# Norm statistics' matmuls between the first pairs' products, operand sums ahead of plain pairs, pools in another order of addresses

## Chip, cores and metric

The kernel runs on one core of one Trainium2 chip. The metric is the device time in microseconds (us); lower is better. TensorE is called PE, VectorE DVE, ScalarE ACT, GpSimd POOL and SyncE SP.

## What is computed

One layer of a decoder trunk over 512 tokens and a width of 1024, in float32: half a SwiGLU feed-forward block (FFN1), token mixing by a convolution branch and a spatial-gating branch, cross-attention over 256 memory tokens, half a second feed-forward block (FFN2), and a final norm.

```python
def rms_norm(x, g):
    xf = x.astype(jnp.float32)
    y = xf * lax.rsqrt(jnp.mean(xf * xf, axis=-1, keepdims=True) + EPS_RMS)
    return (y * g.astype(jnp.float32)).astype(x.dtype)

def swiglu(x, w_gu, w_down):
    gu = x @ w_gu
    g, u = jnp.split(gu, 2, axis=-1)
    return (jax.nn.silu(g) * u) @ w_down
...
  h = x + 1/2 * SwiGLU_1(RMSNorm(x))
  n = RMSNorm(h);  P = n @ W_in + b_in
  A: GLU -> causal depthwise conv (width 31) -> LayerNorm(channels) -> swish -> proj to D
  B: GELU -> split u,v -> LayerNorm(v) -> chunked (128) causal spatial gating u * (W_s v + b), 4 head groups -> proj to D
  merge: sigmoid(gate_A) * y_A + sigmoid(gate_B) * y_B  -> W_out
  h = h + merged
  h = h + CrossAttn(RMSNorm(h), RMSNorm_mem(mem))
  h = h + 1/2 * SwiGLU_2(RMSNorm(h))
  y = RMSNorm_final(h)
```

## The kernel before

**Number format.** The hidden state `h` lies in SBUF, channels on partitions: 8 tiles of 128 channels x 512 tokens. A float32 operand is split into a high part and a low remainder in a shorter format: the high part is a cast on ACT, the low part a subtraction on DVE (`split`, `split_scaled`, lines 190 to 196, and line 110 for weights). One product of the mathematics is then three matmuls (`mm3`, lines 116 to 119: high x high, high x low, low x high), so "a product" below means one of these 128x512 matmuls. Names that end in h and l are the two parts.

**The norms.** `rstat` (lines 211 to 231) makes a norm's factor. ACT squares each tile of `h` and DVE adds it into `acc` (`add_square`, line 204). On PE, n?c (line 218) sums `acc` over channels, as tokens on partitions; DVE adds epsilon (n?m, line 220); POOL takes the power -1/2 (n?r, line 208); DVE scales an identity by it (n?d, line 224); on PE, n?b (line 226) spreads the factors over all partitions; ACT copies them to SBUF (n?rb, line 230). The question mark is 1 in FFN1, 2 ahead of the mixing stage, 3 ahead of the attention, 4 in FFN2. Each n? therefore makes PE wait for DVE, POOL and DVE between its two matmuls, unless other products stand there.

**An FFN.** The width of 2816 is worked in 22 blocks: 6 plain ones (`plain_up`, line 290, `pl` the gate and up sums, `pw0` to `pw5` the weights) and 16 by a Strassen-like scheme of fewer products (`double_f`), whose operands (`operands`) are sums of quarters of the normed x. The first two plain blocks (in FFN1 called `f`, with weights `fw`) are multiplied on x before its norm, and rb is applied to their sums afterwards (`plain_f`, with rb, lines 302 to 309); the others take the normed x (`normed`, line 329: `xf`, `xg`, `lb`, then their split into `xh` and `xl`). In FFN1 the squares are summed after the first blocks' products were issued; in FFN2 `rstat` for n4 is called once after the attention and again inside `ffn`.

**The middle.** Memory keys (`pk`, `kt`), the n2 norm, the conv branch's projections (`av`, `ag`) and its convolution in steps on DVE (line 606), the gating branch, values (`pv`), the branch outputs (`ya`, from `aa`, and `yb`), `w_out` (sums `o`, line 805 adds them to `h`), n3, then queries (`pq`), scores, weighted values and `w_o` (`wo`, line 888). Linear layers fetch weights through a ring (`wpool`) and split them.

**What sets the order.** A scheduler at build time orders the instructions of each engine by its own model of their times, under the data's dependences, the tile pools (a tile of a ring waits for the readers of the one it replaces) and the stages: `stage` opens a list of pools, one behind the other in address, and a tile of a new pool waits only for the old tiles that lay at its addresses. The order of the list therefore decides what a stage's first loads and casts wait for. The middle has one pool `big` of 50 tiles of 128x512 for everything. PSUM has 6 banks for products and 2 for the small ones (n?c, n?b). Each engine's instructions, and SP's DMA issues, run in the order given.

Of the kernel before, what the change touches and what calls it, by code (L numbers as in the profile page):

```python
# [54 lines left out]
def conformer_layer(ctx: ExitStack, tc: tile.TileContext, xT, memT, vecs, rows, w_gp1, w_gs1, w_dn1, w_in_f, w_in_t,  # L55
# [22 lines left out]
    per.tile([P, 24], F32, name="fill")  # L78
# [156 lines left out]
    def slot(name, dt=F32):  # L235
        return pool["big"].tile([P, T], dt, tag="s", name=name, bufs=50)

    def pair(name):
        return slot(name + "h", F32R), slot(name + "l", F32R)
# [6 lines left out]
    FFN_POOLS = ("xops", "wp", "wt", "wr", "wtt", "fp", "tmp")  # L246
# [232 lines left out]
    def ffn(firsts, g, acc, nm, w_gp, w_gs, w_dn, done, last=None):  # L479

        tf, pf = t8("xf"), pt6("xg", F32)
        _, rb = rstat([acc], T, EPS_RMS, nm)
# [12 lines left out]
        if NPL // 2 - 1 in after:  # L495
            down(w_dn, after[NPL // 2 - 1], fs, lambda m: None)
        for d in range(NPL // 2, FT // 2):
            fs[d] = new_f(d)
# [277 lines left out]
    for i in range(DT):  # L776
# [81 lines left out]
    def transposed(pr):  # L858
        out = []
        for j in range(MT):  # L860
# [8 lines left out]
    def weighted(hd, p):  # L869
        for i in range(HT):  # L870
# [170 lines left out]
```

## Time and profile before

| quantity | value |
|---|---|
| median of 3 runs | 1358.31 us (1355.76 to 1358.43) |
| the profiled execution's own time | 1357.26 us |
| its span | 1355.5 us |
| PE busy in the span | 1298.0 us, 96% |
| DVE busy | 903.0 us, 67% |
| ACT busy | 610.9 us, 45% |
| POOL busy | 63.3 us, 5% |
| mean granted clock of PE | 0.975 |

The span is cut from the profiled execution; 1.8 us of its time lie around it. Busy times are sums over instructions. The granted clock is 1 at PE's full speed. A row of a timeline gives the start, the duration, the engine and line, what was written from what, and in brackets how long the engine had been idle and what released it. A matmul's listed duration overlaps with the next one's, so the pace is read from one start to the next.

### The profile page before, as it was taken

To read this page: it belongs to the slowest core of one execution; us is meant where nothing else is said; L and a number is where in the kernel's file an instruction comes from. 1 tells how busy PE (TensorE), PEld (TensorE's weight loads), DVE (VectorE), ACT (ScalarE), POOL (GpSimd) and SP (SyncE) were. 2 spreads that over 40 slices of the span, in tenths; PEclk is the share of its full clock that TensorE was granted. 3 is DMA by queue.
4 is the path that set the end of the run, shared out by engine and by line. 5 is a ranking of instruction groups with operands and counts; after the bars stand their busy time and mean duration, and the time that the engine had idled before them with its cause. 6 is when DMAs were issued, how large, how long until landed. Compare 5 with 4: busy or idle time off the path is not lost.

```text
span 1355.5 us, 17560 instructions
## 1 busy us (share of the span) xinstructions
PE 1298.0 (96%) x7082; PEld 1124.8 (83%) x7082; DVE 903.0 (67%) x1285; ACT 610.9 (45%) x837; POOL 63.3 (5%) x80
## 2 busy tenths in 40 slices
PE   7799999999989999999999999999879999999996
PEld 5589898989878888888888788887658899999995
DVE  4656575665577999999986785555444647575645
ACT  6454554545443223243225643334345455455533
POOL 1000000000020000100000000000111000000000
PEclk9799999999999999999999999999879999999998
DMA  8465565565443222332333333202355546574631
GB/s 250 103 166 131 145 160 163 133 172 129 150 149 116 94 94 95 101 108 80 94 106 113 94 120 96 64 24 67 124 125 125 171 110 172 128 182 130 165 93 62
DMA packets 39809, 166.19 MB, mean 123 GB/s; under 512 B 4337, under 2 KB 7153, under 8 KB 34353
## 3 DMA queue, kind: packets, MB, share of 16 engines
q1 hardware_dynamic: 32096, 129.17, 30.1%
q0 software_dynamic: 7632, 35.92, 13.9%
q8 instruction: 55, 0.90, 0.3%
q14 instruction: 26, 0.20, 0.0%
HBM read 162.97 MB, written 2.10 MB: 122 GB/s over the span
## 4 chain that ended last, share of the span: by engine, by line
PE 74%; issue 14%; DMA 6%; DVE 3%; ACT 2%; POOL 0%; SPq 0%; POOLq 0%; DVEq 0%; ACTq 0%
PE d L117 3%; PE d L118 3%; PE d L119 3%; PE r L186 2%; PE r L187 2%; PE r L185 2%; PE pl L118 2%; PE pl L119 2%; PE pl L117 2%; PE av L118 1%; PE ya L118 1%; PE ya L117 1%; PE av L119 1%; PE ya L119 1%; PE yb L117 1%
## 5 line engine op out<-in xcount | busy, mean ns | idle before, releaser
L606 DVE SCALAR_TENSOR_TENSOR cv<-ap,vec,cv 128x497 f32<-128x497 f32 (+27 forms) x240 | 163.9, 730 | 1.3 <-ACT cv L604 0.9
L242 DVE SCALAR_TENSOR_TENSOR h<-d,h 128x512 f32<-128x512 f32 x79 | 53.8, 687 | 22.8 <-PE d L119 22.2
L203 ACT ACTIVATE sq<-h 128x512 f32<-128x512 f32 x34 | 21.0, 623 | 25.7 <-DVE h L242 16.4
L312 DVE TENSOR_TENSOR u<-pl,g 128x512 f32<-128x512 f32 x8 | 5.5, 690 | 31.8 <-PE pl L119 31.8
L204 DVE TENSOR_TENSOR acc<-acc,sq 128x512 f32<-128x512 f32 x34 | 23.3, 686 | 4.1 <-ACT sq L203 3.7
L196 DVE SCALAR_TENSOR_TENSOR xl<-h,vec,xh 128x512 fp32r<-128x512 f32 x16 | 11.4, 744 | 5.4 <-ACT xh L195 5.4
L117 PE MATMUL pl<-xh,pw20h 128*128 128x512 f32 x16 | 8.6, 563 | 6.4 <-ACT xh L191 6.4
L220 DVE TENSOR_SCALAR n4m<-n4c 128x4 f32<-128x4 f32 x2 | 0.3, 157 | 21.4 <-PE n4c L218 21.4
L805 DVE TENSOR_TENSOR h<-o,h 128x512 f32<-128x512 f32 x8 | 5.5, 692 | 12.5 <-PE o L119 12.5
L794 DVE TENSOR_TENSOR ga<-ya,sga 128x512 f32<-128x512 f32 x8 | 5.5, 690 | 11.9 <-PE ya L119 11.9
L192 DVE TENSOR_TENSOR s40tl<-s40t,s40th 128x1024 fp32r<-128x1024 f32 x4 | 4.9, 1226 | 12.6 <-ACT s40th L191 12.6
L192 DVE TENSOR_TENSOR s60tl<-s60t,s60th 128x1024 fp32r<-128x1024 f32 x4 | 4.9, 1225 | 12.5 <-ACT s60th L191 12.5
L888 DVE TENSOR_TENSOR h<-wo,h 128x512 f32<-128x512 f32 x8 | 5.4, 688 | 11.6 <-PE wo L119 11.6
L192 DVE TENSOR_TENSOR dn40l<-dn,dn40h 128x768 fp32r<-128x768 f32 x4 | 3.8, 959 | 13.2 <-ACT dn40h L191 13.2
L192 DVE TENSOR_TENSOR s80tl<-s80t,s80th 128x1024 fp32r<-128x1024 f32 x4 | 4.9, 1226 | 11.6 <-ACT s80th L191 11.6
L192 DVE TENSOR_TENSOR s100tl<-s100t,s100th 128x1024 fp32r<-128x1024 f32 x4 | 4.9, 1225 | 11.4 <-ACT s100th L191 11.4
L117 PEld LDWEIGHTS pl<-xh,pw20h 128*128 128x128 f32 x16 | 4.3, 281 | 9.8 <-ACT xh L191 8.9
L191 ACT CAST s31th<-s31t 128x1024 fp32r<-128x1024 f32 x4 | 4.2, 1052 | 17.5 <-PE d L118 17.5
L117 PE MATMUL pl<-xh,pw30h 128*128 128x512 f32 x16 | 7.4, 490 | 4.6 <-DVE g L306 4.6
L195 ACT ACTIVATE xh<-h,vec 128x512 fp32r<-128x512 f32 x16 | 10.9, 713 | 1.4 <-PE wo L119 0.9
L191 ACT CAST fh<-u 128x512 fp32r<-128x512 f32 x12 | 7.4, 618 | 8.8 <-DVE u L309 8.8
L118 PE MATMUL pl<-xl,pw20h 128*128 128x512 f32 x16 | 8.2, 515 | 3.1 <-DVE xl L192 3.1
(3770 smaller groups left out, 5072.3 us busy)
## 6 DMA issues: line engine op xcount, KB each, us to landing
s<-w_gs SPq DMA_DIRECT2D x32, 1024.0 KB, 5.6
dn<-w_dn SPq DMA_DIRECT2D x32, 512.0 KB, 3.9
pw<-w_gp SPq DMA_DIRECT2D x10, 1024.0 KB, 5.1
dn<-w_dn SPq DMA_DIRECT2D x8, 768.0 KB, 5.0
h<-xT SPq DMA_DIRECT2D x8, 256.0 KB, 7.4
first<-w_gp SPq DMA_DIRECT2D x4, 512.0 KB, 7.6
r10w<-w_in_t SPq DMA_DIRECT2D x4, 512.0 KB, 3.7
r11w<-w_in_t SPq DMA_DIRECT2D x4, 512.0 KB, 3.8
```

Of the source, the lines that this page charges most:

```text
L117: PE.matmul(out, whi, ahi, start=start, stop=False)
L118: PE.matmul(out, whi, alo, start=False, stop=False)
L119: PE.matmul(out, wlo, ahi, start=False, stop=stop)
L185: PE.matmul(accs[t], a_h, whi[:, k - k0, :], start=k == 0, stop=False)
L186: PE.matmul(accs[t], a_h, wlo[:, k - k0, :], start=False, stop=False)
L187: PE.matmul(accs[t], a_l, whi[:, k - k0, :], start=False, stop=k == nk - 1)
L191: S.copy(out=hi, in_=src)
L192: V.tensor_tensor(out=lo, in0=src, in1=hi.bitcast(F32), op=ALU.subtract)
L203: S.activation(sq, src, AF.Square)
L204: V.tensor_tensor(out=acc, in0=acc, in1=sq, op=ALU.add)
L242: V.scalar_tensor_tensor(out=h[:, m, ts], in0=pd, scalar=0.5, in1=h[:, m, ts], op0=ALU.mult, op1=ALU.add)
L606: V.scalar_tensor_tensor(out=o, in0=aps[i][:, :T - back], scalar=w, in1=o, op0=ALU.mult, op1=ALU.add)
```

## The change

It splits `rstat` in two, `rstat_cols` (n?c to n?d) and `rstat_rows` (n?b and its copy), so that products can stand between them. In FFN1 the squares are added inside the loop over channels, n1c comes ahead of the last channel tile's products, n1b between the two blocks of the last tile, and a third plain block (`pw2`) is multiplied on the x before its norm. In FFN2, n4c goes between the two halves of the first plain block and n4b between those of the second, and the other call for n4 is dropped. The operands' sums are made ahead of the first plain block that takes the normed x, no longer behind it. The middle's pools are regrouped: `xp`, `kv` (8 tiles for keys, values, csum and later the probabilities) and `tmp` live through the whole middle; `mixing` (`big` with 34 tiles, `mp` with 8, `wpool`) is closed after n3 and `attention` (`big` with 26, `late` with 16, `wpool`) opened in its place. The FFN's pools get an order each.

```diff
-    def rstat(accs, n, eps, name, copy=True):
+    def rstat_cols(accs, n, eps, name):
...
+        return rc, dg
+
+    def rstat_rows(dg, n, name, copy=True):
+
         pb = ps2.tile([P, T], F32, tag="st", name=name + "b")[:, :n]
         PE.matmul(pb, ones, dg, start=True, stop=True)
...
-    FFN_POOLS = ("xops", "wp", "wt", "wr", "wtt", "fp", "tmp")
+
+    FFN1_POOLS = ("wr", "fp", "wtt", "tmp", "xops", "wp", "wt")
+    FFN2_POOLS = ("wp", "fp", "tmp", "wr", "wtt", "xops", "wt")
...
-    def plain_up(w_gp, j, xh, xl, by_dma):
+    def plain_up(w_gp, j, xh, xl, by_dma, between=None):
...
             plain_mm(accs, w, xh, xl, kh, range(4))
+            if kh == 0 and between is not None:
+                between()
         return accs
...
-        fs = {0: new_f(0)}
-        for j in range(2):
-            plain_f(firsts[j], rb, fs[0], j)
-        for j in range(2, NPL):
+        fs = {}
+        ops = None
+        for j in range(NPL):
             if j % 2 == 0:
                 fs[j // 2] = new_f(j // 2)
+            if j < len(firsts):
+                plain_f(firsts[j], rb, fs[j // 2], j % 2)
+                continue
+            if ops is None:
+                ops = operands(x, src)
             plain_f(plain_up(w_gp, j, xh, xl, True), None, fs[j // 2], j % 2)
-            if j == 2:
-                ops = operands(x, src)
...
+            if k == DT - 2:
+                add_square(acc, h[:, k + 1, :], False)
+                dg = rstat_cols([acc], T, EPS_RMS, "n1")[1]
             for j in range(2):
                 plain_mm(firsts[j], ws[j], xh, xl, kh, (0, 1) if kk == 1 else (kk,))
-        acc = new_acc("acc0")
-        for k in range(DT):
-            add_square(acc, h[:, k, :], k == 0)
+                if k == DT - 1 and j == 0:
+                    rb = rstat_rows(dg, T, "n1")
+        firsts.append(plain_up(w_gp1, 2, xh, xl, True))
...
-    stage(middle, ("wpool", "xp", "big", "tmp"), 5)
+    stage(middle, ("xp", "kv", "tmp"), 5)
+    mixing = ExitStack()
+    stage(mixing, ("big", "mp", "wpool"), 5)
+    SLOTS.update(big=34, mp=8, kv=8)
...
     rc, rb = rstat([acc], T, EPS_RMS, "n3")
     acc = new_acc("acc3")
 
+    mixing.close()
+    attention = ExitStack()
+    stage(attention, ("big", "late", "wpool"), 5)
+    SLOTS.update(big=26, late=16)
...
-    _, rb = rstat([acc], T, EPS_RMS, "n4")
+    attention.close()
     middle.close()
...
-        firsts = [plain_up(w_gp2, j, xh, xl, False) for j in range(2)]
+        stat = []
+        firsts = [plain_up(w_gp2, 0, xh, xl, False, lambda: stat.append(rstat_cols([acc], T, EPS_RMS, "n4")[1]))]
+        firsts.append(plain_up(w_gp2, 1, xh, xl, False, lambda: stat.append(rstat_rows(stat[0], T, "n4"))))
+        rb = stat[1]
```

What the scheduler makes of it is shown at three places. In the rows x4 is a count, and what stands in front of MATMUL is the line.

**PE in FFN1, at n1.** Before, n1c and n1b stand side by side behind the last `f`:

```order
L118 MATMUL f_126<-xl_107,fw11h 128x512
L119 MATMUL f_126<-xh_104,fw11l 128x512
L218 MATMUL n1c<-avg,acc_255 128x1 x4
L226 MATMUL n1b<-n1d,ones 128x512
L117 MATMUL pl_347<-xh_300,pw20h 128x512
L117 MATMUL pl_348<-xh_300,pw20h 128x512
L117 MATMUL pl_455<-xh_300,pw30h 128x512
L117 MATMUL pl_456<-xh_300,pw30h 128x512
L118 MATMUL pl_347<-xl_301,pw20h 128x512
```

With the change, n1c stands 24 products ahead of the last `f`:

```order
L118 MATMUL f_126<-xl_106,fw11h 128x512
L119 MATMUL f_126<-xh_103,fw11l 128x512
L218 MATMUL n1c<-avg,acc_127 128x1 x4
L117 MATMUL f_123<-xh_104,fw01h 128x512
L118 MATMUL f_123<-xl_107,fw01h 128x512
```

and n1b stands behind the fifth product of the third block:

```order
L119 MATMUL f_126<-xh_104,fw11l 128x512
L117 MATMUL pl_298<-xh_101,pw20h 128x512
L118 MATMUL pl_298<-xl_105,pw20h 128x512
L119 MATMUL pl_298<-xh_101,pw20l 128x512
L117 MATMUL pl_298<-xh_101,pw20h 128x512
L118 MATMUL pl_298<-xl_105,pw20h 128x512
L230 MATMUL n1b<-n1d,ones 128x512
L119 MATMUL pl_298<-xh_101,pw20l 128x512
```

n1c and n1b now have 24 and 5 products between them; before they had none, and 43 products of the third block follow n1b before the first normed xh.

**PE and DVE where the attention begins.** Before, PE goes from the last `o` to `pq`; n3c stands further on, among the products of `pq0` and `pq1`. DVE makes the low parts of `pq2` and `pq3` there:

```order
L118 MATMUL o_6926<-mg7l,o7w0h 128x512
L119 MATMUL o_6926<-mg7h,o7w0l 128x512
L117 MATMUL pq_7014<-xhi,pq0w0h 128x512
L118 MATMUL pq_7014<-xlo,pq0w0h 128x512
L119 MATMUL pq_7014<-xhi,pq0w0l 128x512
```

```order
L805 TENSOR_TENSOR h<-o_6926,h 128x512
L110 TENSOR_TENSOR pq2w0l<-pq2w_7089,pq2w0h 128x1024
L196 SCALAR_TENSOR_TENSOR xlo<-h,vec,xhi 128x512
L204 TENSOR_TENSOR acc_6699<-acc_6699,sq 128x512
L110 TENSOR_TENSOR pq3w0l<-pq3w_7170,pq3w0h 128x1024
L220 TENSOR_SCALAR n3m<-n3c 128x4
```

With the change, n3c stands ahead of `pq`, and on DVE the low parts of the keys (`k0l`, `k1l`) ahead of the last `xlo` and `acc`:

```order
L118 MATMUL o_6934<-mg7l,o7w0h 128x512
L119 MATMUL o_6934<-mg7h,o7w0l 128x512
L218 MATMUL n3c<-avg,acc_6707 128x1 x4
L117 MATMUL pq_7034<-xhi,pq0w0h 128x512
L118 MATMUL pq_7034<-xlo,pq0w0h 128x512
L119 MATMUL pq_7034<-xhi,pq0w0l 128x512
```

```order
L830 TENSOR_TENSOR h<-o_6934,h 128x512
L192 TENSOR_TENSOR k0l<-kt_3400,k0h 128x512
L192 TENSOR_TENSOR k1l<-kt_3515,k1h 128x512
L196 SCALAR_TENSOR_TENSOR xlo<-h,vec,xhi 128x512
L204 TENSOR_TENSOR acc_6707<-acc_6707,sq 128x512
L192 TENSOR_TENSOR k2l<-kt_3580,k2h 128x512
L110 TENSOR_TENSOR pq0w0l<-pq0w_7035,pq0w0h 128x1024
L220 TENSOR_SCALAR n3m<-n3c 128x4
```

n3c moved ahead of the 35 products of `pq` that stood in front of it; the keys' and the values' splits, which on DVE followed the last `mg` early in `w_out`'s products, came behind the last `h`, and so did `pq0`'s.

**PE from `w_o` into FFN2.** Before, the first n4c stands between the last `wo` and the first `pl`:

```order
L118 MATMUL wo_7919<-oo7l,wo7w0h 128x512
L119 MATMUL wo_7919<-oo7h,wo7w0l 128x512
L218 MATMUL n4c<-avg,acc_6981 128x1 x4
L117 MATMUL pl_8022<-xh_7997,pw00h 128x512
L118 MATMUL pl_8022<-xl_8001,pw00h 128x512
L117 MATMUL pl_8023<-xh_7997,pw00h 128x512
```

With the change it stands behind 29 products of `pw0`, and n4b behind 43 more:

```order
L118 MATMUL pl_8026<-xl_8006,pw01h 128x512
L119 MATMUL pl_8026<-xh_8003,pw01l 128x512
L117 MATMUL pl_8026<-xh_8003,pw01h 128x512
L118 MATMUL pl_8026<-xl_8006,pw01h 128x512
L218 MATMUL n4c<-avg,acc_6989 128x1 x4
L119 MATMUL pl_8026<-xh_8003,pw01l 128x512
```

```order
L118 MATMUL pl_8101<-xl_8006,pw10h 128x512
L119 MATMUL pl_8101<-xh_8002,pw10l 128x512
L230 MATMUL n4b<-n4d,ones 128x512
L117 MATMUL pl_8100<-xh_8003,pw11h 128x512
L118 MATMUL pl_8100<-xl_8006,pw11h 128x512
```

The second pair of n4c and n4b, which stood behind all 96 products, is gone; 24 products follow n4b before the first normed xh.

## Rows read from the trace of the kernel before

**Rows 1.** Page, sections 1 and 6: PE's busy time; the pw loads.

```profile
PE 1298.0 (96%) x7082; PEld 1124.8 (83%) x7082; DVE 903.0 (67%) x1285; ACT 610.9 (45%) x837; POOL 63.3 (5%) x80
...
pw<-w_gp SPq DMA_DIRECT2D x10, 1024.0 KB, 5.1
```

**Rows 2.** Waits of PE: engine line <- releaser: us in total, times, longest.

```profile
PE pl L117 <- ACT xh L191: 6.4, 2, 3.2
PE n4c L218 <- DVE acc L204: 6.1, 1, 6.1
PE pl L117 <- DVE g L306: 4.6, 2, 2.3
...
PE n1b L226 <- DVE n1d L224: 2.9, 1, 2.9
...
PE n4b L226 <- DVE n4d L224: 2.4, 1, 2.4
...
PE pk L117 <- ACT m0h L195: 1.9, 1, 1.9
PE ya L117 <- ACT aa0h L191: 1.9, 1, 1.9
```

**Rows 3.** Stretches: us; busy us (xcount) of PE, PEld, DVE, ACT, POOL; PEclk, DMA share, GB/s.

```profile
30.90:51.90 21.00, 11.09 (x28) 6.73 (x27) 15.51 (x26) 10.90 (x14) 2.83 (x3) 0.59 0.57 142
...
376.20:412.00 35.80, 30.04 (x184) 26.83 (x184) 28.63 (x54) 17.99 (x33) 7.57 (x11) 0.86 0.55 176
...
440.00:714.50 274.50, 274.41 (x1269) 228.50 (x1268) 260.01 (x378) 87.76 (x110) 4.29 (x5) 1.00 0.31 95
...
752.20:760.00 7.80, 5.92 (x18) 4.15 (x17) 6.56 (x10) 7.80 (x14) 0.00 (x0) 0.78 0.73 217
...
962.80:1015.00 52.20, 36.63 (x133) 27.84 (x132) 26.38 (x43) 22.65 (x28) 7.61 (x6) 0.77 0.56 155
```

**Rows 4.** Timeline of PE, FFN1's norm: start us, us, engine line op [idle before <-releaser].

```profile
30.65 0.39 PE L119 MATMUL f<-xh,fw11l 128*128 128x512 f32 x1
30.88 0.95 PE L218 MATMUL n1c<-avg,acc 128*128 128x1 f32 x8
34.73 2.00 PE L226 MATMUL n1b<-n1d,ones 128*128 128x512 f32 x2 [2.90 <-DVE n1d L224]
...
46.35 0.80 PE L118 MATMUL pl<-xl,pw20h 128*128 128x512 f32 x1 [1.53 <-DVE xl L192]
46.95 0.63 PE L119 MATMUL pl<-xh,pw20l 128*128 128x512 f32 x1
47.37 0.63 PE L117 MATMUL pl<-xh,pw20h 128*128 128x512 f32 x1
```

**Rows 5.** Timeline of DVE, same stretch.

```profile
20.61 0.68 DVE L204 TENSOR_TENSOR acc<-acc,sq 128x512 f32<-128x512 f32 x1
...
37.38 2.74 DVE L329 SCALAR_TENSOR_TENSOR xf<-h,vec,n1rb 128x512 f32<-128x512 f32 x4 [2.71 <-ACT n1rb L230]
...
45.08 2.35 DVE L192 TENSOR_TENSOR xl<-xf,xh 128x1024 fp32r<-128x1024 f32 x2
```

**Rows 6.** Timeline of PE, from the attention's last product into FFN2.

```profile
962.78 0.39 PE L119 MATMUL wo<-oo7h,wo7w0l 128*128 128x512 f32 x1
...
1010.77 0.79 PE L118 MATMUL pl<-xl,pw20h 128*128 128x512 f32 x1 [1.53 <-DVE xl L192]
```

**Rows 7.** Line 208 (POOL): duration ns min/median/max, first and last start.

```profile
L208 POOL TENSOR_TENSOR n4r<-n4m,vec x2: 1030/2010/2990, 972.3 to 997.8; 128x4 f32<-128x4 f32 x2
...
L208 POOL TENSOR_TENSOR n2r<-n2m,vec x1: 1009/1009/1009, 393.3 to 393.3; 128x4 f32<-128x4 f32 x1
```

**Rows 8.** Timeline of PE where pq begins.

```profile
843.42 0.39 PE L117 MATMUL pq<-xhi,pq0w0h 128*128 128x512 f32 x1
```

**Rows 9.** Timeline of DVE at the last h of the mixing stage.

```profile
843.62 0.69 DVE L805 TENSOR_TENSOR h<-o,h 128x512 f32<-128x512 f32 x1 [2.05 <-PE o L119]
...
846.33 0.68 DVE L204 TENSOR_TENSOR acc<-acc,sq 128x512 f32<-128x512 f32 x1
```

More of the change, by code (lines that the diff above doesn't have):

```diff
@@ L76, in conformer_layer @@
     G.memset(mhalf, -0.5)
-    per.tile([P, 24], F32, name="fill")
+    per.tile([P, 8], F32, name="fill")
     pool = {}
@@ L227, in rstat, with slot, pair @@
         if not copy:
-            return rc, pb
+            return pb
         rb = per.tile([P, n], F32, tag=f"rb{n}", name=name + "rb", bufs=1)
         S.copy(out=rb, in_=pb)
-        return rc, rb
+        return rb
+    def rstat(accs, n, eps, name, copy=True):
+        rc, dg = rstat_cols(accs, n, eps, name)
+        return rc, rstat_rows(dg, n, name, copy)
     def new_acc(name):
         return per.tile([P, T], F32, tag="acc", name=name, bufs=1)
[L235 to L239, printed above, removed]
+    SLOTS = {}
+    def slot(name, dt=F32, of="big"):
+        return pool[of].tile([P, T], dt, tag="s", name=name, bufs=SLOTS[of])
+    def pair(name, of="big"):
+        return slot(name + "h", F32R, of), slot(name + "l", F32R, of)
     def add_half(m, pd, ts=slice(0, T)):
         V.scalar_tensor_tensor(out=h[:, m, ts], in0=pd, scalar=0.5, in1=h[:, m, ts], op0=ALU.mult, op1=ALU.add)
-    FFN_POOLS = ("xops", "wp", "wt", "wr", "wtt", "fp", "tmp")
+    FFN1_POOLS = ("wr", "fp", "wtt", "tmp", "xops", "wp", "wt")
+    FFN2_POOLS = ("wp", "fp", "tmp", "wr", "wtt", "xops", "wt")
     def raw2(name):
@@ L505, in conformer_layer @@
     with ExitStack() as stack:
-        stage(stack, FFN_POOLS, 7)
+        stage(stack, FFN1_POOLS, 7)
         HF = DT // 2
@@ L520, in conformer_layer @@
         ws = {}
+        acc = new_acc("acc0")
         for k in range(DT):
             split_scaled(xh[k], xl[k], h[:, k, :], col("ffn1_norm", k))
+            if k < DT - 1:
+                add_square(acc, h[:, k, :], k == 0)
             kh, kk = k // HF, k % HF
@@ L564, in mem_operands @@
             if k % 2 == 0:
-                hi, lo = pair(f"m{k0 + k}")
+                hi, lo = pair(f"m{k0 + k}", "mp")
             c = slice(k % 2 * NM, (k % 2 + 1) * NM)
@@ L632, in conformer_layer @@
                     channel_multiplier=-1)
-    wsh, wsl = pair("ws")
+    wsh, wsl = pair("ws", "kv")
     split(wsh, wsl, wsr)
@@ L660, in norm_v @@
         for t in range(TT):
-            st = pool["tmp"].tile([P, 2, 6], F32, tag="st6", name="st", bufs=2)
+            st = pool["tmp"].tile([P, 2, 6], F32, tag="st6", name="st", bufs=1)
             for half in range(2):
@@ L664, in norm_v @@
                 yield OP_US
-            mv = pool["tmp"].tile([P, 2], F32, tag="mv", name="mv", bufs=2)
+            mv = per.tile([P, 2], F32, tag="mv", name="mv", bufs=2)
             V.bn_aggr(out=mv, in_=st)
@@ L718, in value @@
         for t in range(MT):
-            vts[t][half] = slot(f"vt{half}{t}")
+            vts[t][half] = slot(f"vt{half}{t}", of="kv")
             S.activation(vts[t][half], accs[t], AF.Copy, scale=mrc[:, t:t + 1])
@@ L782, in conformer_layer @@
         V.tensor_tensor(out=y, in0=y, in1=sg, op=ALU.mult)
-        hi, lo = pair(f"aa{i}")
+        hi, lo = pair(f"aa{i}", "mp" if i < 4 else "big")
         split(hi, lo, y)
@@ L863, in transposed @@
                 PE.transpose(pt[:, t * P:(t + 1) * P], pr[t][:, j * P:(j + 1) * P], ident)
-            hi, lo = pair("p")
+            hi, lo = pair("p", "kv")
             split(hi, lo, pt)
@@ L875, in weighted @@
                 mm3(po, vh[j][k // 4][:, kc], vl[j][k // 4][:, kc], p[j][0], p[j][1], j == 0, j == MT - 1)
-            hi, lo = pair(f"oo{k}")
+            hi, lo = pair(f"oo{k}", "late")
             split(hi, lo, po)
@@ L916, in conformer_layer @@
         attn_out(m, 0, 8)
-    _, rb = rstat([acc], T, EPS_RMS, "n4")
+    attention.close()
     middle.close()
     with ExitStack() as stack:
-        stage(stack, FFN_POOLS, 7)
+        stage(stack, FFN2_POOLS, 7)
         xh, xl = plain_x()
```

15 lines of the change are left out of this document (7 added, 8 removed).

## The prediction

> **What bounds the kernel now.** I read the page first: TensorE (PE) is busy for 1298.0 of 1355.5 us [rows 1], so what can be won is what PE still waits, and what it does at half clock. Next the waits of PE [rows 2]: the reader is to see that the long ones sit in few places. The two FFNs' norms have xh (6.4 us, two waits), g (4.6, two), n4c (6.1), n1b (2.9) and n4b (2.4); besides, pk waits 1.9 for m0h and ya 1.9 for aa0h. Third, the stretches [rows 3]. Where PE waited, its clock fell from 1.00 to a mean of 0.59 (30.9 to 51.9 us) or 0.77 (962.8 to 1015): PE ran there partly at 1.2 instead of 2.4 GHz. Between 440 and 714.5 us it lacks nothing. Last the timelines: a product of 128x512 follows the one before after 0.23 us at full clock and after 0.42 us at half [rows 4].
>
> **FFN1's norm (n1).** Now PE stands from n1c at 30.88 to the first xl product at 46.35 with little to do [rows 4]: 15.5 us, in which its own work is n1c 0.95, n1b about 1.0 (it took 2.00 at half clock) and four products by 0.23, so 2.9. In the change n1c stands 24 products earlier, at 30.88 - 24 x 0.23 = 25.4. Its sum is ready at 20.61 + 0.68 = 21.3 [rows 5], so it does not wait. From n1c's end to n1b was 2.9 us [rows 4]; n1b now has 29 products in front of it (6.7 us), so it doesn't wait either and starts at 25.4 + 0.95 + 6.7 = 33.0. From n1b's start to the first xl took 11.6 us, 10.6 without the 1.0 that n1b ran long. That makes 43.6. PE meanwhile has n1b, 43 products of the third pair (9.9) and the four xh products: 44.8. So xl is there first, by 1.2 us; the chain xf to xl on VectorE (DVE), 37.38 to 45.08 [rows 5], lies beside the third pair. Wait gained: 15.5 - 2.9 = **12.6**. The half clock goes with it: 46.35 to 51.9 ran at half, 5.5 us, half of which is **2.8**. The third pair's two more multiplications by rb are DVE work in a stretch where DVE has 5.5 us idle [rows 3], and cost nothing; without that cover they cost two instructions like acc's, 1.4. Together **-15.4**.
>
> **FFN2's norm (n4).** From the last product of w_o, 962.78 + 0.23 = 963.0, to the first xl product at 1010.77 [rows 6] are 47.8 us. In the change PE goes straight from w_o into pw0, n4c stands behind 29 products, at 963.0 + 6.7 = 969.7. The last sum into acc, which came 6.1 us late [rows 2] behind a run of xl on DVE, stands in the new order right behind the last h, xl and squares being spread over w_o's last products. n4c takes 0.95, 43 products 9.9, so n4b starts at 980.5; the chain's 2.9 is covered. The second n4c and n4b, and their waits, are gone. After n4b PE has 1.0 + 24 x 0.23 + 4 x 0.23 and is through at 987.9. The normed xl comes 10.6 after n4b's start, and n4rb stands behind the casts of pw3 on ScalarE (ACT), about 0.7 more (an estimate from half of the queue that the order shows): 991.8. So there remains a wait of some 3.9, most of it the four products' on xh, g and xl, and a stretch at half clock behind it as now. 991.8 against 1010.77 is **-19.0**; with no wait at all it would be -22.9, with the queue's whole two casts in the way -17.5.
>
> **Where the attention begins.** Here the change adds a wait. pq starts now at 843.42 without one [rows 8]. In the new order n3c stands ahead of the first pq, and the sum that it needs is behind more work: DVE has k0l, k1l (their tiles lie in the pool opened only here), then xlo, then acc. The last h is added at 843.62 and takes 0.69 [rows 9]; four instructions of about 0.6 behind it end at 846.7. PE idles from 843.4 to 846.7, 3.3 us. pq0w0h is cast behind the last xhi, square and k2h, and its low half behind that, so the third product waits another 0.5 or so. What is behind n3c in PE's queue is all of pq. n3c itself only moves. After such waits half clock follows: in 752.2 to 760, behind a wait of 1.9, the mean is 0.78, so (1 - 0.78) / 0.5 x 7.8 = 3.4 us at half, 1.7 lost [rows 3]; I take 1.9 here. Sum **+5.7**; the ends are 3.3 (no fall of the clock) and 9 (a clock loss as long as that of 376.2 to 412, below).
>
> **Into the middle, and pv to ya.** From 376.2 to 412 PE lacks 35.8 - 30.0 = 5.8 us, and at mean clock 0.86 it loses 5.0 more [rows 3]. mem's casts and squares now stand ahead of the last down casts, so pk's 1.9 goes [rows 2] with some 1.7 of clock; in return d waits for its own casts about 1.5, and n2c, now directly behind nmb, leaves n2b little cover of its 2.9 us chain, 1.1 more. **-1.0**, between -5 (most of the 10.8 gone) and +3 (every wait comes back longer). At ya, aa0h moves up on ACT: 0.5 of its 1.9 goes, and the clock's 1.7: **-2.2**, between 0 and -3.6.
>
> Weighed at n2b: POOL's power (line 208) took 1.03 us for one n4r and 2.99 for the other, and 1.01 for n2r [rows 7]. Between n2's mean and its diagonal the new order has only the kt products on DVE, which read PSUM; I take 1.0, and the other end adds 2.0. The Trainium skill (SBUF — State Buffer, § Who interferes with whom) says that a DVE instruction with two SBUF inputs and a GpSimd one that reads SBUF shut each other out; kt has one such input, so by it, too, n2r stays short, and the sum would be as here; by the 2.99 of the trace it would be 2.0 higher.
>
> **The rest.** The products' number is the same but for the duplicate statistics. Sizes and order of pools leave FFN bodies and tail as they are; the operands' sums ahead of pw3 are DVE work with the plain pairs over it. 0.
>
> **Sum:** -15.4 - 19.0 + 5.7 - 1.0 - 2.2 = **-31.9**. The profiled execution took 1357.26 (span 1355.5 and 1.8 around it); that makes 1325.4. The median shown is 1.05 above that execution, so **1326**.
>
> **Rivals.**
> 1. *Loads come late.* The pools opened for the attention and FFN2 lie over tiles in use until just before. pw0's load is now queued on SP ahead of w_o's last, and its cast ahead of two w_o casts on ACT; if its tile comes free late, all three wait. Price: a load, 5.1 [rows 1], and clock of 1.9, in one place: 1333; in both 1340. For it: the load waits for PE. Against it: w_o's last four products, 4 x 24 x 0.23 = 22 us, run meanwhile. Chance 0.15.
> 2. *The new waits are cheaper.* No clock loss at pq (-1.9) and the middle's better end (-4): 1320. Chance 0.15.
> 3. *Slower: the mixing stage starves.* It keeps 34 shared tiles and 8 for mem and aa where 50 were. If a tile that a gate or a projection needs comes free only when the conv is through, DVE stands and the sums behind it come late. DVE is busy 260.0 of 274.5 us there [rows 3], and PE is at its limit, so the first few us are hidden. To end slower by 0.2% DVE would have to idle 35 us more than now, a busy share under 0.84 instead of 0.95 in that stretch: 1361. Against it: the same instructions stand there, and conv steps come earlier than now against v's norm. Chance 0.03.
> 4. *The norm's gain is given back* by one miss in both FFNs, for instance PSUM banks freed late by g and u: 30 us back, no change, 1357. Chance 0.02.
>
> **How the numbers follow.** 0.65 for the forecast, with bounds of its own terms of 1320 to 1332. 1316 to 1340 takes in both nearer rivals and the terms' ends. About 0.2% (2.7 us) is what a measurement of this kernel can tell from no change: faster 0.95, same 0.02, slower 0.03.
>
> **What would show it.** Right: n1c and n1b wait for nothing, clock 1.00 from 31 to 52 us; one n4c and one n4b, without waits; one new wait of PE, n3c on acc, near 3.3 us; about 4 us left in FFN2's xh, g, xl. Wrong: a wait of wo or pq on a weight cast; DVE below 0.84 in the conv; pl of FFN1 waiting for xl.

## The result and the profile after

The change takes 1321.34 us, median of 4 runs (1318.53 to 1323.13), against 1358.37 for the kernel before (4 runs, 1355.76 to 1359.5): the ratio is 0.973, 95% interval 0.971 to 0.975, so 37.0 us less. The forecast was 1326: 31.9 less than the profiled execution of before, and 1.05 added because the median of before lay above that execution. The profiled execution of the change took 1321.24, with a span of 1319.1.

The page's line of the engines, after (against [rows 1]: PE has 14 us less busy time for all but ten of the same matmuls; some 2 us of that are the ten, the second n4c and n4b, and the rest goes with the mean granted clock, which rose from 0.975 to 0.988):

```profile
PE 1284.0 (97%) x7072; PEld 1117.5 (85%) x7072; DVE 903.5 (68%) x1282; ACT 610.5 (46%) x836; POOL 59.8 (5%) x79
```

First, where the gain arises. These are rows of PE's timeline before: the last product of FFN1's plain blocks (`pl`, called FFN1's last up product below), the first `av`, the first `ya`, the last `o`, the last `pl` of FFN2 (FFN2's last up product) and the last 512-column product of its down sums `d`. The last `wo` stands in [rows 6]:

```profile
91.47 0.39 PE L119 MATMUL pl<-xh,pw51l 128*128 128x512 f32 x1
...
402.26 0.50 PE L117 MATMUL av<-xhi,av0w0h 128*128 128x512 f32 x1 [1.54 <-ACT xhi L191]
...
754.46 0.50 PE L117 MATMUL ya<-aa0h,yaw0h 128*128 128x512 f32 x1 [1.88 <-ACT aa0h L191]
...
843.19 0.39 PE L119 MATMUL o<-mg7h,o7w0l 128*128 128x512 f32 x1
...
1055.02 0.39 PE L119 MATMUL pl<-xh,pw51l 128*128 128x512 f32 x1
...
1335.52 0.39 PE L119 MATMUL d<-fh,dn43l 128*128 128x512 f32 x1
```

and the same after, with the last `wo`:

```profile
76.12 0.39 PE L119 MATMUL pl<-xh,pw51l 128*128 128x512 f32 x1
...
384.55 0.50 PE L117 MATMUL av<-xhi,av0w0h 128*128 128x512 f32 x1 [2.11 <-ACT xhi L191]
...
734.03 0.39 PE L117 MATMUL ya<-aa0h,yaw0h 128*128 128x512 f32 x1
...
822.20 0.39 PE L119 MATMUL o<-mg7h,o7w0l 128*128 128x512 f32 x1
...
946.63 0.39 PE L119 MATMUL wo<-oo7h,wo7w0l 128*128 128x512 f32 x1
...
1019.97 0.39 PE L119 MATMUL pl<-xh,pw51l 128*128 128x512 f32 x1
...
1299.93 0.39 PE L119 MATMUL d<-fh,dn43l 128*128 128x512 f32 x1
```

The differences, from place to place, against the terms of the prediction (negative: earlier with the change, time won):

| up to | after - before, us | of it in this piece | term |
|---|---|---|---|
| FFN1's last up product | -15.35 | -15.35 | -15.4 |
| first `av` | -17.71 | -2.36 | -1.0 |
| first `ya` | -20.43 | -2.72 | -2.2 |
| last `o` | -20.99 | -0.56 | 0 |
| last `wo` | -16.15 | +4.84 | +5.7 |
| FFN2's last up product | -35.05 | -18.90 | -19.0 |
| FFN2's last down product | -35.59 | -0.54 | 0 |
| end of the span (1355.5, 1319.1) | -36.4 | -0.8 | 0 |

The longest waits of PE that are left (engine line <- releaser: us in total, times, longest) follow. Left out are those that the kernel before has too at the start and in the final norm, FFN2's two, whose rows stand further down, and those under 1.4. Against [rows 2], the waits of n4c, n1b and n4b, both on xh, pk's and ya's 1.9 are gone, and one is new, n3c's:

```profile
PE n3c L218 <- DVE acc L204: 3.3, 1, 3.3
...
PE av L117 <- ACT xhi L191: 2.1, 1, 2.1
PE av L118 <- DVE xlo L192: 2.0, 1, 2.0
...
PE n2b L230 <- DVE n2d L224: 1.4, 1, 1.4
```

The stretches after (columns as in [rows 3]; the first is FFN1's norm, the second the way into the middle, the third the conv, the fourth pv to ya, the fifth the start of pq, the sixth FFN2's norm):

```profile
30.90:51.90 21.00, 21.00 (x92) 16.85 (x91) 17.04 (x26) 15.91 (x20) 3.52 (x4) 1.00 0.95 219
362.00:398.00 36.00, 30.48 (x189) 26.87 (x189) 25.16 (x46) 14.12 (x22) 6.81 (x11) 0.91 0.58 176
427.00:702.00 275.00, 275.00 (x1273) 229.24 (x1272) 259.21 (x379) 90.11 (x114) 4.28 (x5) 1.00 0.31 97
732.00:748.00 16.00, 15.23 (x66) 12.04 (x65) 13.63 (x19) 14.80 (x24) 0.00 (x0) 1.00 0.49 138
...
822.40:841.90 19.50, 16.16 (x59) 12.84 (x59) 13.67 (x22) 9.45 (x14) 1.33 (x1) 0.82 0.36 109
...
946.60:980.00 33.40, 30.57 (x123) 23.91 (x122) 16.19 (x28) 16.77 (x20) 4.64 (x5) 0.90 0.57 125
```

FFN1's norm lacks nothing any more: PE is busy for all of 30.9 to 51.9, at clock 1.00 where it was 0.59. The conv's DVE share is 259.2 of 275, 0.94 against 0.95: rival 3 didn't come.

PE at FFN1's norm: n1c, n1b and the first product on the normed x.

```profile
25.48 0.95 PE L218 MATMUL n1c<-avg,acc 128*128 128x1 f32 x8
...
32.97 1.02 PE L230 MATMUL n1b<-n1d,ones 128*128 128x512 f32 x2
...
43.62 0.61 PE L117 MATMUL pl<-xh,pw30h 128*128 128x512 f32 x2
```

The prediction had 25.4 and 33.0 for the first two, and the normed xl ready (43.6) before the third block ends (44.8). No row has an idle time in brackets.

PE from `w_o` into FFN2:

```profile
953.43 0.95 PE L218 MATMUL n4c<-avg,acc 128*128 128x1 f32 x8
...
964.10 1.02 PE L230 MATMUL n4b<-n4d,ones 128*128 128x512 f32 x2
...
972.95 1.39 PE L117 MATMUL pl<-xh,pw30h 128*128 128x512 f32 x2 [1.89 <-DVE g L321]
975.27 0.80 PE L118 MATMUL pl<-xl,pw20h 128*128 128x512 f32 x1 [0.94 <-DVE xl L192]
```

Counted from the end of the last `wo` (946.63 + 0.23 = 946.86): n4c at 6.6 (predicted 6.7), n4b at 17.2 (17.5), the first xl product at 28.4 (28.8).

Where pq begins, on PE, behind the last `o` of 822.20:

```profile
825.92 1.50 PE L218 MATMUL n3c<-avg,acc 128*128 128x1 f32 x8 [3.34 <-DVE acc L204]
827.28 0.77 PE L117 MATMUL pq<-xhi,pq0w0h 128*128 128x512 f32 x1
```

and on DVE, whose `acc` n3c waits for:

```profile
822.62 0.69 DVE L830 TENSOR_TENSOR h<-o,h 128x512 f32<-128x512 f32 x1 [2.61 <-PE o L119]
823.23 0.68 DVE L192 TENSOR_TENSOR k0l<-kt,k0h 128x512 fp32r<-128x512 f32 x1
823.83 0.69 DVE L192 TENSOR_TENSOR k1l<-kt,k1h 128x512 fp32r<-128x512 f32 x1
824.43 0.75 DVE L196 SCALAR_TENSOR_TENSOR xlo<-h,vec,xhi 128x512 fp32r<-128x512 f32 x1
825.09 0.68 DVE L204 TENSOR_TENSOR acc<-acc,sq 128x512 f32<-128x512 f32 x1
```

The wait is 3.34 (predicted 3.3), and the chain is the predicted one.

### The profile page after: what moved, and what is told of

The parts are those of the page before. It is cut to its first block, busy times and chain, and to the rows that moved or that the text cites. A ratio compares the mean times of both kernels' runs of the same rounds, so it can differ in the third digit from the quotient of the medians.

```text
span 1319.1 us, 17537 instructions
## 1 busy us (share of the span) xinstructions
PE 1284.0 (97%) x7072; PEld 1117.5 (85%) x7072; DVE 903.5 (68%) x1282; ACT 610.5 (46%) x836; POOL 59.8 (5%) x79
## 4 chain that ended last, share of the span: by engine, by line
PE 76%; issue 14%; DMA 6%; DVE 3%; ACT 1%; POOL 0%; DVEq 0%; POOLq 0%; SPq 0%
PE d L117 4%; PE d L119 4%; PE d L118 4%; PE r L186 2%; PE r L187 2%; PE r L185 2%; PE pl L118 2%; PE pl L119 2%; PE pl L117 2%; DMA s60pl<-w_gs 1%; PE pq L117 1%; PE av L118 1%; PE pq L118 1%; PE pq L119 1%; PE av L119 1%
## 5 line engine op out<-in xcount | busy, mean ns | idle before, releaser
L631 DVE SCALAR_TENSOR_TENSOR cv<-ap,vec,cv 128x497 f32<-128x497 f32 (+29 forms) x240 | 163.3, 727 | 1.5 <-ACT cv L629 0.9
L191 ACT CAST s31th<-s31t 128x1024 fp32r<-128x1024 f32 x4 | 4.2, 1052 | 17.5 <-PE d L118 17.5
L208 POOL TENSOR_TENSOR rs<-va,vec 128x1 f32<-128x1 f32 x4 | 3.7, 933 | 168.9 <-DVE va L693 168.9
L858 DVE TENSOR_TENSOR qt<-pq,n3rb 128x512 f32<-128x512 f32 x8 | 5.5, 691 | 8.2 <-PE pq L119 8.1
L117 PE MATMUL f<-xh,fw00h 128*128 128x512 f32 x8 | 3.7, 501 | 7.7 <-ACT fw00h L191 7.7
L195 ACT ACTIVATE xhi<-h,vec 128x512 fp32r<-128x512 f32 x8 | 5.8, 720 | 11.5 <-DVE h L830 11.5
L192 DVE TENSOR_TENSOR fl<-u,fh 128x512 fp32r<-128x512 f32 x12 | 8.2, 685 | 3.8 <-ACT fh L191 3.8
L192 DVE TENSOR_TENSOR dn41l<-dn,dn41h 128x768 fp32r<-128x768 f32 x4 | 3.8, 953 | 10.2 <-ACT dn41h L191 10.2
L878 ACT ACTIVATE pr<-sc,mx 128x256 f32<-128x256 f32 x16 | 7.4, 471 | 6.8 <-DVE mx L875 6.8
```

The source lines that it names most:

```text
L117: PE.matmul(out, whi, ahi, start=start, stop=False)
L192: V.tensor_tensor(out=lo, in0=src, in1=hi.bitcast(F32), op=ALU.subtract)
L195: S.activation(hi, src, AF.Copy, scale=g)
L631: V.scalar_tensor_tensor(out=o, in0=aps[i][:, :T - back], scalar=w, in1=o, op0=ALU.mult, op1=ALU.add)
```

## The experiments

Where a run is said to be ahead or late "at the last `o`" or another product, the starts of that product in the profiled executions are compared, as in the table above. PE's first wait, for fw00h, was 6.9 to 8.5 us in these executions, so a difference under 1.5 us at one place says little.

### The three parts alone: e1, e2, e3

e1: FFN1's code alone. The pools, the operands' sums and FFN2 stay as before.

```diff
         for k in range(DT):
...
+            if k < DT - 1:
+                add_square(acc, h[:, k, :], k == 0)
...
+                dg = rstat_cols([acc], T, EPS_RMS, "n1")[1]
...
+                if k == DT - 1 and j == 0:
+                    rb = rstat_rows(dg, T, "n1")
+        firsts.append(plain_up(w_gp1, 2, xh, xl, True))
```

> FFN1's part of the change alone (squares inside the loop, n1c and n1b between products, a third plain pair ahead of the norm), with the pools, the middle and FFN2 as before. Theory (the wait is gone because 29 products stand between n1c and n1b and 43 behind n1b; addresses have no part in it): PE clock 1.00 from 31 to 52 us, FFN1 15.4 us shorter, the rest as before: -15.4 us against before, ratio 0.9887. Rival (the new addresses are needed, since pw2's load or its tiles come free too late in the old order): a wait of PE on pw20h or pw30h in FFN1, less than 10 us won.

Measured: 1336.45 against 1355.83, ratio 0.987 (0.985 to 0.988). At FFN1's last up product it is 15.4 ahead of before, as the change is. n4c's wait of 6.1 stays. Ahead of the first `ya` it gains 6.3 more, though pk's wait is still there; that piece is looked at in the last section.

e2: FFN2's code alone, with the old pools.

```diff
-    _, rb = rstat([acc], T, EPS_RMS, "n4")
...
+        firsts = [plain_up(w_gp2, 0, xh, xl, False, lambda: stat.append(rstat_cols([acc], T, EPS_RMS, "n4")[1]))]
+        firsts.append(plain_up(w_gp2, 1, xh, xl, False, lambda: stat.append(rstat_rows(stat[0], T, "n4"))))
```

> FFN2's code alone (n4 once, n4c and n4b inside the first two pairs), with the pools and FFN1 as before. Theory (what starts the pairs early is the order of addresses, not the code): n4c still stands right behind the last wo and still waits 6 us on acc, with half clock behind it; the second n4c and n4b and their 2.4 us go, and the chain behind n4b is partly covered: -8.5 us, ratio 0.9937. Rival (the code alone moves the statistics): the whole -19.

e3: the pools alone, with the old code of both norms.

```diff
+    FFN1_POOLS = ("wr", "fp", "wtt", "tmp", "xops", "wp", "wt")
+    FFN2_POOLS = ("wp", "fp", "tmp", "wr", "wtt", "xops", "wt")
...
+    stage(middle, ("xp", "kv", "tmp"), 5)
+    stage(mixing, ("big", "mp", "wpool"), 5)
...
+    stage(attention, ("big", "late", "wpool"), 5)
```

> The pools alone (the three stages' order of addresses, the middle regrouped), with n1, n4 (twice) and the operands' sums as before. Theory: at FFN2 the wait of 6.1 on acc and its half clock go (about -10), where the attention begins n3c waits 3.3 with half clock behind (+5), ahead of the projections and at ya some 5 are won: -10, ratio 0.993. Rival (addresses hardly matter, the code of the norms does it all): within 3 us of before.

Measured: e2 1343.88, ratio 0.991 (0.989 to 0.993); e3 1345.36, ratio 0.993 (0.991 to 0.994). e2's profiled execution took 1347.31, 3.4 more than its median. Between the last `wo` and FFN2's last up product e2 gains 10.3 and e3 8.9; the change gains 18.9. So that term has two halves of nearly equal size. What each half is, the rows show. In e2, which has FFN2's new code, n4c still stands right behind the last `wo`, on PE:

```profile
962.87 0.39 PE L119 MATMUL wo<-oo7h,wo7w0l 128*128 128x512 f32 x1
969.36 1.84 PE L218 MATMUL n4c<-avg,acc 128*128 128x1 f32 x8 [6.11 <-DVE acc L204]
```

It waits as in the kernel before, because `acc` stands behind seven xl on DVE:

```profile
963.90 4.71 DVE L196 SCALAR_TENSOR_TENSOR xl<-h,vec,xh 128x512 fp32r<-128x512 f32 x7
```

In e3, which has the old code, n4c stands behind 29 products of `pw0`, as in the change, and waits for nothing:

```profile
960.25 0.39 PE L119 MATMUL wo<-oo7h,wo7w0l 128*128 128x512 f32 x1
...
967.06 0.95 PE L218 MATMUL n4c<-avg,acc 128*128 128x1 f32 x8
```

and the last `acc` on DVE ends 2.3 behind the last `wo`, where it ends 6.1 behind it in e2:

```profile
962.13 0.69 DVE L204 TENSOR_TENSOR acc<-acc,sq 128x512 f32<-128x512 f32 x1 [0.76 <-ACT sq L203]
```

So it is the pools, and not the new code, that put products ahead of n4c and `acc` early. With the new addresses pw0's first cast starts at 938.2 in e3, 22 us ahead of the last `wo`'s end; with the old ones it starts at 965.6 in e2, 2.5 behind it, so that no product on it could follow the last `wo` directly. FFN2's code gives the other half: the second n4c and n4b are gone, and n4b stands behind 72 products instead of 28, so that it and FFN2's xh are waited for no longer. e3 also has the new n3c wait of 3.3, and loses 4.7 between the last `o` and the last `wo` as the change does (4.8): that loss belongs to the pools.

The three spans are 20.5, 9.9 and 11.6 shorter than before, 42.0 together against the change's 36.4. The difference lies in the middle: up to the last `o` e1 gains 6.2 beyond FFN1, e3 7.1, and the change 5.6. e1's edit touches nothing there, and its gain is in large part clock (last section); that the change could not win this on top of e3's is argued, not shown.

### Two un-normed blocks in FFN1: e4

```diff
-        firsts.append(plain_up(w_gp1, 2, xh, xl, True))
```

> The change without the third plain pair ahead of n1. Theory (that pair is the cover of the chain from n1b to the normed xl, 10.6 us): PE waits about 9 us on xh, g and xl in FFN1 again, half clock behind it costs some 3 more: 1332 us, 11 us above the change. Rival (n1c's early place won the time, the pair only moved work): within 3 us of the change.

Measured: 1333.47, ratio 0.984 (0.983 to 0.985). FFN1's last up product is only 1.4 ahead of before; 13.9 of the 15.4 are gone, or 13.1 of 15.8 if one counts from PE's first product, which came 0.8 later in e4 than in the change. PE in FFN1, where the third block's products were:

```profile
38.56 1.22 PE L117 MATMUL pl<-xh,pw20h 128*128 128x512 f32 x2 [4.54 <-ACT xh L191]
...
42.06 1.40 PE L117 MATMUL pl<-xh,pw30h 128*128 128x512 f32 x2 [2.28 <-DVE g L321]
...
45.65 0.79 PE L118 MATMUL pl<-xl,pw20h 128*128 128x512 f32 x1 [2.20 <-DVE xl L192]
```

Moving n1c and n1b takes away their own 2.9, but the chain behind n1b (rb, xf, xh, xl) is as long as ever, and PE waits for it at the next place. The cover of 48 more products (the third block) is what wins the time.

### The wait ahead of pq: e5, e6

e5: one weight ring for the whole middle, opened ahead of the mixing stage, so that pq0's load and casts need not wait for a pool opened only there. To make room, the orders of the FFNs' pools change too.

```diff
-    FFN1_POOLS = ("wr", "fp", "wtt", "tmp", "xops", "wp", "wt")
+    FFN1_POOLS = ("wr", "fp", "tmp", "xops", "wtt", "wp", "wt")
...
-    stage(middle, ("xp", "kv", "tmp"), 5)
+    stage(middle, ("xp", "kv", "tmp", "wpool"), 5)
...
-    stage(mixing, ("big", "mp", "wpool"), 5)
+    stage(mixing, ("big", "mp"), 5)
...
-    stage(attention, ("big", "late", "wpool"), 5)
+    stage(attention, ("late", "big"), 5)
```

> The change with the weight ring (wpool) opened once for the whole middle instead of anew for the attention, and the FFN's pools put in an order that fits. Theory (the wait of n3c comes from the ring that was opened anew: pq's first casts must wait until w_out is through, so pq can't go ahead of n3c): PE goes from the last o straight into pq, n3c stands among pq's products and waits for nothing, no half clock there: 4.9 us below the change, 1316.5, ratio 0.969. Rival (the keys' splits ahead of xlo and acc on DVE make the wait): the 3.3 us stay, 1321.

Measured: 1321.15, ratio 0.974 (0.972 to 0.976): no different from the change, a miss for the 1316.5 of theory, and yet the wait is gone. PE goes from the last `o` into pq:

```profile
826.39 0.39 PE L119 MATMUL o<-mg7h,o7w0l 128*128 128x512 f32 x1
826.62 0.39 PE L117 MATMUL pq<-xhi,pq0w0h 128*128 128x512 f32 x1
```

From the last `o` to the end of pq0 it wins 4.8 on the change, what theory gave. But it came to `o` 4.2 late: n2b now waits 4.0, where the change has 1.4. In this layout the squares of the memory are summed later on DVE (nmc at 376.6 instead of 370.2), and all of kt's six multiplications, 2.07 us, then stand between n2's mean and its diagonal. The loss is not in the place that the edit was for, but in another whose tiles share the same addresses; whether FFN1's order or the ring's place puts the squares later was not separated.

e6: the keys' and values' splits written behind the first query, to see whether k0l and k1l make the wait.

```diff
+    fill(0)
     kh, kl = [], []
...
-    for i in range(3):
+    for i in range(1, 3):
```

> The change with the keys' and values' splits written behind the first query. Theory (the ring makes the wait, two splits of 0.6 only lengthen it): n3c waits about 2.1 instead of 3.3, half clock behind it stays: 1 to 1.5 us below the change, ratio about 0.972. Rival (the splits are the cause): the whole 4.9 go, ratio 0.969.

Measured: 1322.26, ratio 0.975 (0.973 to 0.976); n3c waits 3.0 instead of 3.3. Neither theory's 2.1 and its gain of 1 to 1.5 came, nor the rival's 4.9: without the keys ahead of it, `acc` is hardly earlier. In the change's trace ACT makes the square that `acc` adds from 823.98 to 824.59, behind xhi (823.35) and the last `h`; so `acc` can't start before 824.6, against 825.09, and only 0.5 of the 3.3 is the keys'. Nor would n3c further back have won the rest: ACT casts pq0w0h from 825.00 to 826.04, and the first pq needs it, 3.6 behind the last `o`'s end. e5 takes both away: its cast stands early, and pq ahead of n3c.

### A third un-normed block in FFN2: e7, e9

```diff
         firsts.append(plain_up(w_gp2, 1, xh, xl, False, lambda: stat.append(rstat_rows(stat[0], T, "n4"))))
+        firsts.append(plain_up(w_gp2, 2, xh, xl, True))
```

> The change with a third plain pair ahead of the norm in FFN2 too, as FFN1 has it. Theory (what is left at n4 is a chain of 10.6 us behind n4b with 24 products as cover): the waits of 1.9 on g and 0.9 on xl go, and with them half clock of 6.8 us, 3.4 lost: 6 us below the change, ratio 0.968. Rival (pw2's weights, made by a DMA with accumulation, or the PSUM banks then come late): a new wait on pw20l or g, no gain.

Measured: 1315.96, ratio 0.970 (0.969 to 0.972), FFN2's last up product 6.3 earlier than in the change. The stretch of FFN2's norm:

```profile
946.60:980.00 33.40, 33.40 (x151) 27.43 (x150) 16.26 (x27) 18.58 (x22) 5.43 (x6) 1.00 0.59 126
```

The 2.8 that PE lacked are gone and the clock is 1.00 instead of 0.90. This is what the prediction called the 3.9 that remain, with their half clock.

e9 is e5 and e7 together:

> Both of the two above together. Theory: their gains add up, 4.9 + 6: 1310.5, ratio 0.965. Rival: one of them is only moved (half clock falls elsewhere), 1315.

Measured: 1315.35, ratio 0.970 (0.968 to 0.971), no better than e7, so theory's 1310.5 was missed and its rival came: e5's 4.8 at pq are paid for ahead of `av` again (+5.3 at the last `o`).

### The operands' sums: e8

```diff
-            if ops is None:
-                ops = operands(x, src)
             plain_f(plain_up(w_gp, j, xh, xl, True), None, fs[j // 2], j % 2)
+            if ops is None:
+                ops = operands(x, src)
```

> The change with the operands' sums behind the first plain pair that takes the normed x, as before. Theory (the sums are DVE work that products cover in either place): within 2 us of the change, 1321, ratio 0.973. Rival (ahead of the pair they bring the Strassen products' operands earlier, or behind it they let xl through sooner): more than 2 us either way.

Measured: 1319.91, ratio 0.973 (0.971 to 0.975). That part of the change makes no difference that can be measured.

### Better versions: e10, e11, e12

e10: e7, and n2's statistics ahead of the memory's norm, to take away n2b's and av's waits in the middle. e11 is e10 with e5's ring.

```diff
+    dg2 = rstat_cols([acc], T, EPS_RMS, "n2")[1]
+    rb = rstat_rows(dg2, T, "n2")
     for k0 in range(0, DT, HF):
         mem_operands(k0)
...
-            _, rb = rstat([acc], T, EPS_RMS, "n2")
```

> The change with FFN2's third pair, and n2's statistics issued ahead of the memory norm's, so that the keys' products stand between n2c, n2b and the first av. Theory (what is left ahead of the projections is the same kind of wait as at n1 and n4, 1.4 + 2.1 + 1.3 and half clock of 6.8 us behind it): some 7 us below the third pair's 1316, 1309, ratio 0.965. Rival (the memory norm's chain is now the last one, and av waits for a PSUM bank that kt frees): 1314.

> The same with the one weight ring. Theory (what the one ring lost ahead of the projections, n2b's 4.0 and half clock, was n2's place): the 4.8 won at pq now count, 1304.5, ratio 0.961. Rival (the loss comes from the new order of FFN1's addresses): as without the ring, 1309, or above.

Measured: e10 1313.81, ratio 0.968 (0.967 to 0.970); e11 1311.40, ratio 0.967 (0.965 to 0.968). Both miss their theories (1309 and 1304.5); for e10 the rival came. n2b and xhi are waited for no longer, but `av` then waits in both for kt, which frees its PSUM bank:

```profile
PE av L117 <- DVE kt L609: 4.5, 1, 4.5
```

On DVE in e11, kt stands behind five xn, a weight's low part and an xlo, none of which stands ahead of kt in the change:

```profile
383.33 3.39 DVE L617 SCALAR_TENSOR_TENSOR xn<-h,vec,n2rb 128x512 f32<-128x512 f32 x5
...
388.38 2.07 DVE L609 TENSOR_TENSOR kt<-pk,nmrb 128x256 f32<-128x256 f32 x6
```

With the ring the memory's sums come later again (nmc at 380.4 in e11, 376.5 in e10), so what e5 lost ahead of `av` was not only n2's place: of the 4.8 that e11 wins at pq, 2.5 are gone at the last `o`.

e12 tests that reading: e7, with n2c ahead of the memory's matmul nmc, and n2b right behind nmb, so that four kt come before xn.

```diff
+    dg2 = rstat_cols([acc], T, EPS_RMS, "n2")[1]
     mrc, mrb = rstat([macc], NM, EPS_RMS, "nm")
...
-            _, rb = rstat([acc], T, EPS_RMS, "n2")
+            rb = rstat_rows(dg2, T, "n2")
```

> The change's pools, the third pair in FFN2, and n2 between the two of memory's norm: n2c ahead of memory's, n2b behind nmb, with 32 products of 256 columns (3.8 us) behind it before the first av. In the run with n2 first, PE lost a wait of 4.5 us for kt and about 3.4 us of clock where av begins, because kt's multiplications stood behind five xn on VectorE. Theory (that order on VectorE is the cause): here four kt stand ahead of xn, so av waits neither for kt nor for n2b; of the change's 1.4 (n2b), 2.1 (xhi), 2.0 (xlo) and 3.4 (clock) there, 5 to 9 go: against the third pair alone (1316.0 with a before of 1356.9) 1307 to 1311. Rival (the wait moves on once more: xn, now behind four kt and a cast, is late, and av waits 3 us or more for xhi or xlo, with half clock): 1313 to 1316.

Measured: 1310.62 against 1357.24, ratio 0.966 (0.964 to 0.967). On DVE four kt stand ahead of xn:

```profile
375.77 1.41 DVE L608 TENSOR_TENSOR kt<-pk,nmrb 128x256 f32<-128x256 f32 x4 [0.69 <-ACT nmrb L234]
377.10 3.50 DVE L617 SCALAR_TENSOR_TENSOR xn<-h,vec,n2rb 128x512 f32<-128x512 f32 x5
```

`av` waits no longer for kt nor for n2b; 1.3 is left for xlo and 0.6 for a cast. The last `o` is 5.9 ahead of e7's, within the 5 to 9 that theory gave. e12 and e11 are the fastest, not to be told apart; both beat the change. e12 still has n3c's wait of 3.3; e12 with e5's ring was not tried.

## Why the prediction was right, point by point

**FFN1's norm** (-15.4): -15.35, or -15.8 from PE's first product, which came 0.4 later with the change. Every step of it stands in the trace, and e1 shows that FFN1's code alone gives it. e4 shows the step that carries it: the third block as the cover of n1b's chain.

**FFN2's norm** (-19.0): -18.9. The size came out because the working followed the new order on every engine, with `acc` "right behind the last h". The prediction didn't say what put n4c and `acc` there; e2 and e3 show that it is the pools (8.9), and that the new code without them wins 10.3 and leaves n4c and its wait where they were. One end of that term is worked out wrongly: twice the 0.7 taken for half of ACT's queue gives -18.3, not -17.5; the forecast doesn't use it.

At n2b the prediction took 1.0 for POOL's n2r, not 2.99. Measured (duration in ns, then the start), and what DVE did meanwhile:

```profile
L208 POOL TENSOR_TENSOR n2r<-n2m,vec x1: 1007/1007/1007, 378.8 to 378.8; 128x4 f32<-128x4 f32 x1
```

```profile
378.63 1.07 DVE L607 TENSOR_TENSOR kt<-pk,nmrb 128x256 f32<-128x256 f32 x3
```

n2r ran beside kt, whose one SBUF input is nmrb, and took 1.01. The Trainium skill (SBUF — State Buffer, § Who interferes with whom), by which such an instruction doesn't shut POOL out, agrees with this row. The one n4r that is left took 1.34.

**Where the attention begins** (+5.7): +4.84. The wait is right, and so is its chain on DVE. Three sizes inside the sum were off and nearly cancel, which is luck. The clock cost more than the 1.9 taken: in 822.4 to 841.9 its mean is 0.82, so (1 - 0.82) / 0.5 x 19.5 = 7.0 us ran at half, 3.5 lost. That is this execution's: in e4 and e8, with the same wait, the mean is 0.91, half as much is lost, and the piece is +3.2. The 0.5 for the third product didn't come at all: pq0's low half is made while n3c and the first products run. And 1.2 came back that was not in the sum: po waits 1.1 for ph where it waited 2.3. These give 3.3 + 3.5 - 1.2 = 5.6; the remaining 0.8 to the measured 4.84 was not traced.

**Into the middle** (-1.0): -2.36, inside its ends of -5 and +3. Two of its three parts were right (pk's wait goes; n2b now waits 1.4, predicted 1.1). The third, d waiting 1.5 for its casts, didn't come: in the change PE's waits show none. PE lacks 36.0 - 30.5 = 5.5 us in 362 to 398 against 5.8 in the stretch of before, and loses (1 - 0.91) x 36 = 3.2 to the clock against 5.0: so the gain there is clock, not wait.

**pv to ya** (-2.2, end -3.6): -2.72, and more. The wait fell from 1.9 to 0.8 (for aa0l; 0.5 had been predicted to go), and the clock's 1.7 went with it: 732 to 748 has 1.00. Part of both lies behind the first `ya`, in the next piece of the table: there the kernel before ran at half clock until 758.5, and the change has its 0.8. The -0.56 of that piece belongs here, then; every run with the new pools has -0.53 to -0.59 there, and e1 and e2, with the old ones, +0.1. Together that is -3.3, still short of the end of -3.6.

**The rest** (0): the -0.54 in FFN2's body is within what executions differ by (from -1.0 to +1.3 in the runs above). The last -0.8 is the end, behind the last down product, where half clock lasts a little shorter in this execution.

**The sum** was 4.5 too small: 1.4 in the middle, 1.1 at ya, 0.9 at pq, 0.5 in FFN2's body and 0.8 at the end, all to the same side, less 0.1 in FFN2's norm. Rival 2, the cheaper waits, thus came about in part in the middle (-2.4 where it had -5), but not at pq, where the clock did fall. Rival 1 (loads late) didn't come: PE's waits name no weight of `wo`, `pq` or `pl`, but for 0.2 for wo4w0l, as before the change. One weight was late all the same, hidden behind n3c's wait: pq0w0h, whose cast ended at 826.04. Rival 4 would show in xh, g or xl in both FFNs; FFN1 has none of them, FFN2 2.8.

## What to carry to other kernels

When a reduction's matmul is moved ahead among other products, count the whole chain behind it up to the first instruction that needs its result: moving the matmul wins its own wait, and only products that don't need the result win the rest (here 13 of some 15 us in FFN1, and 6.3 more in FFN2). Look also at which tiles lie at the same addresses: half of FFN2's gain came from the pools, and a pool order that took away a wait of 3.3 at one place made one of 4.0 at another. After each wait removed, ask which engine's queue holds the next: kt became the last wait only when n2's had gone.

## What was not expected of the hardware

The same short waits cost clock in one run and none in another. The kernel before has 0.86 in 376.2 to 412 [rows 3], behind pk's wait of 1.9 and av's two of 1.5 and 2.0. e2, with the same three waits, has 0.95 in 378 to 414. e1 has the same pk wait, then one of 0.5 for a cast and one of 1.2 for xlo, and no fall at all:

```profile
360.50:397.00 36.50, 32.49 (x211) 28.57 (x210) 28.91 (x54) 18.07 (x33) 6.66 (x11) 1.00 0.52 174
```

e1's further gain of 6.3 ahead of `ya` is in large part the 5.0 of clock that the kernel before lost there. At pq the wait is 3.3 in the change and in e8; the change has 0.82 behind it, e8 0.91 in a stretch of the same length:

```profile
822.00:841.50 19.50, 16.16 (x67) 12.86 (x67) 14.91 (x24) 11.03 (x16) 3.06 (x1) 0.91 0.36 109
```

What decides between the two isn't shown here. In such a place the clock term of a forecast is a chance, not a number; the range should hold both.

POOL's power for the memory's norm, nmr, took 0.72 us in the change and 1.68 in e11, where it started at 381.2 beside ag0w0l on DVE (381.12, 1.23 us, two inputs in SBUF) and ended half a microsecond behind it: the lengthening that [rows 7] has for n4r, on another instruction. There the 2.99 started at 972.3, beside pw10l (972.06) and pw11l (973.19) on DVE, 1.2 us each and again with two inputs in SBUF.
